# A hybrid DeltaNet and attention layer: the second set of inverse loads placed behind the gates' tenth store on SP's queue

## The chip, the cores and the metric

The kernel runs on one core of one Trainium2 chip. The metric is the device time of the launch in microseconds (us): lower is better. The time before is the median of three runs.

## The reference

One layer over 2048 latent tokens of width 1024 and 256 context tokens. A normed, modulated input `h` goes through one wide projection. Two mixers run side by side: a bidirectional chunked gated DeltaNet (4 heads of 128) and windowed attention (8 heads of 64). Each has a SiLU gate (`za`, `zb`), the two are merged by sigmoid gates (`ga`, `gb`) and projected once more.

```python
a_mat = where(strict, einsum('nbhik,nbhjk->nbhij', kb, kc) * decay, 0)
t_mat = triangular_solve(a_mat, eye, lower=True, unit_diagonal=True)   # one inverse for each chunk, head, direction
u = einsum('nbhij,nbhjv->nbhiv', t_mat, vc * bc)
w = einsum('nbhij,nbhjk->nbhik', t_mat, kb * exp(gc))
s_fin, o = lax.scan(step, s0, (u, w, k_dec, g_last, qk, q_dec))        # one state step per chunk, both directions
y = (sigmoid(ga) * (ya @ w_proj_a) + sigmoid(gb) * (yb @ w_proj_b)) @ w_out
```

What matters here is `t_mat`, the inverse of a unit lower triangular matrix for each chunk of 64 tokens, and the gate projections `za`, `zb`, `ga`, `gb`, which are large matrix products that depend on none of that.

## The kernel before

Products are done in a split form: each f32 operand is a high part (`wh`, `hh`) and the rest (`wl`, `hl`), and three matmuls for each of 8 slices of 128 add up to one product, so one product of the gates is 24 matmuls of 128x512.

**The gates.** `gates(range(24), (2, 3), ...)` runs over 24 column tiles m of the gate weights (m below 4 is `za`, below 8 `zb`, below 16 `ga`, the rest `gb`), and for each m over the token groups 2 and 3. In this document product n is the one with n = 2m for group 2 and n = 2m + 1 for group 3. `rest` loads and splits the weights of the next m (`wr` by SP, L241; `wh` on ScalarE, L243; `wl` on VectorE, L246). `rest_run` does product n into one of three PSUM banks (L524 to L526), takes a tanh on ScalarE into one of two SBUF buffers `rt` (L816), and for m below 8 multiplies on VectorE (L818), which is what frees the bank, and stores `rt` from SP's queue (L819). So product n + 3 needs the bank that L818 of product n frees, and the tanh of product n + 2 needs the buffer that store n has left.

**The inverses.** `base` runs twice. Each call loads a set of raw triangular blocks into `N`, 64 partitions for each direction (`nb` at L733, `N` at L734, both on SP's queue; `N` is 1 MB a direction), scales them by beta on VectorE (L737 for the forward half, L739 for the backward half, four instructions each), runs 62 steps of two VectorE instructions each (L747, L749), clears the upper parts on GpSimd (L754) and stores the result (L759). The first set has the context chunks, the first latent blocks of the forward order and the first of the backward one; the second set has the middle blocks, which the scan comes to after eight steps. The steps of both sets share one buffer `btmp`, so the second set's steps run after the first set's. The first set's loads are three `nb` and `N` pairs, since its chunks are not all neighbours; the second set's are two pairs. `base4` does the last blocks, later, and uses the second set's `N` and `nb` again. `mod_gate` sums the residual gate beside the gates: loads `wmg` on SP (L220), scaling on ScalarE (L221), sums on GpSimd (L223).

**What sets the order.** The order of each engine's queue here is made at build time from a simulated timeline: an instruction is put on its engine when the simulation has it ready, the earlier traced first. On the chip each queue then runs in that order. `tc.issue_after(i)` adds no wait: it keeps the instructions of its block behind `i` on `i`'s engine.

Of the kernel before, what the change touches and what calls it, by code (L numbers as in the profile page):

```python
# [32 lines left out]
def hybrid(tc, ins, out, dbg=None, upto=9):  # L33
    nc = tc.nc
    V, S, G, T = nc.vector, nc.scalar, nc.gpsimd, nc.tensor
    ctx = ExitStack()
    with ctx:
        _hybrid(ctx, tc, nc, V, S, G, T, ins, out, dbg, upto)


def _hybrid(ctx, tc, nc, V, S, G, T, ins, out, dbg, upto):
    dma = nc.sync.dma_start
    adma = nc.scalar.dma_start
# [4 lines left out]
    def dscr(name, shape, dt=F32):  # L48
        return dram.tile(shape, dt, name=name)

    def mem(tag):
        if dbg is not None:
            print("MEM", tag, tile.free_sbuf_bytes_per_partition(tc))
# [44 lines left out]
    Nsp = [dscr(f"Nsp{d}", [NC, H, 2, 64, 64]) for d in range(2)]  # L98
    offsp = [dscr(f"offsp{d}", [NC, 64, H, 64]) for d in range(2)]
    QDsp = dscr("QDsp", [NB, 128, H, 128])  # L100
    brT = dscr("brT", [NC, 8, 128])
# [47 lines left out]
    def acc(shape, dt=F32, name="acc"):  # L149
        return psum("acc", shape, dt, name)  # L150
# [101 lines left out]
    if True:  # L252
# [46 lines left out]
        for j in range(2):  # L299
            mps = [psum("acc" if n == 0 else "hps", [4, 512], name=f"mps{n}") for n in range(2)]  # L300
            for k in range(KT):
# [10 lines left out]
                if j == 0 and 2 <= k < 2 + NCB:  # L312
                    c = k - 2
# [169 lines left out]
        for gi in range(8):  # L483
            xts = []
            for j in range(2):
                c = NCB + gi * 2 + j
# [9 lines left out]
            c = NCB + gi * 2  # L496
# [24 lines left out]
    def fm_dense(ps, w, xh, xl, kt=KT):  # L521
        wh, wl = w
        for k in range(kt):
            T.matmul(ps, lhsT=wh[:, k], rhs=xh[:, k], start=k == 0, stop=False)  # L524
            T.matmul(ps, lhsT=wh[:, k], rhs=xl[:, k], start=False, stop=False)  # L525
            T.matmul(ps, lhsT=wl[:, k], rhs=xh[:, k], start=False, stop=k == kt - 1)  # L526
# [183 lines left out]
    def runs(chunks):  # L710

        out = []
        for i, c in enumerate(chunks):
            if out and c == out[-1][1] + out[-1][2]:
                out[-1][2] += 1
            else:
                out.append([i, c, 1])
        return out

    def base(si, npool, pool, fr, bk):  # L720


        n = 8 * len(fr)
        h1 = max(32, n)
        N = npool.tile([128, 64, 64], F32, name="N")
        nb = npool.tile([128, 64], F32, name="nb")
        if n < h1:
            G.memset(N[0:h1], 0.0)
            G.memset(nb[0:h1], 0.0)
        for d, chunks in ((0, fr), (1, bk)):  # L730
            for i0, c, k in runs(chunks):
                p0 = d * h1 + i0 * 8
                dma(nb[p0:p0 + 8 * k], brT[c:c + k, d * 4:d * 4 + 4].rearrange("c h (b t) -> c (h b) t", b=2))  # L733
                dma(N[p0:p0 + 8 * k], Nsp[d][c:c + k].rearrange("c h b r i -> (c h b) r i"))  # L734
        for q in range(4):
            r, w = slice(q * 16, q * 16 + 16), q * 16 + 16
            V.tensor_tensor(N[0:h1, r, 0:w], N[0:h1, r, 0:w],  # L737
                            nb[0:h1, 0:w].unsqueeze(1).to_broadcast([h1, 16, w]), op=ALU.mult)
            V.tensor_tensor(N[h1:h1 + n, r, 0:w], N[h1:h1 + n, r, 0:w],  # L739
                            nb[h1:h1 + n, r].unsqueeze(2).to_broadcast([n, 16, w]), op=ALU.mult)  # L740
        yield 9
        A = N[0:h1 + n]
        for m in range(1, 63):
            tmp = pool.tile([128, 1376], F32, name="btmp")
            r = 63 - m
            tv = tmp[0:h1 + n, :r * m].rearrange("p (r j) -> p r j", j=m)
            V.tensor_tensor(tv, A[:, m + 1:, m].unsqueeze(2).to_broadcast([h1 + n, r, m]),  # L747
                            A[:, m, 0:m].unsqueeze(1).to_broadcast([h1 + n, r, m]), op=ALU.mult)
            V.tensor_tensor(A[:, m + 1:, 0:m], A[:, m + 1:, 0:m], tv, op=ALU.add)  # L749
            yield 2 * (65 + 1.04 * r * m) / 1e3  # L750

        for q in range(4):
            r, w = slice(q * 16, q * 16 + 16), 64 - q * 16
            G.affine_select(A[:, r, q * 16:], A[:, r, q * 16:], pattern=[[1, 16], [-1, w]], base=0,  # L754
                            channel_multiplier=0, compare_op=ALU.is_gt, fill=0.0)
        V.memset(A.rearrange("p r c -> p (r c)")[:, ::65], 1.0)
        for d, chunks in ((0, fr), (1, bk)):
            p0 = d * h1
            dma(Xset[d][si].rearrange("c h b r j -> (c h b) (r j)"), N[p0:p0 + n].rearrange("p r j -> p (r j)"))  # L759
            for ci, c in enumerate(chunks):  # L760
                Xsp[d][c] = Xset[d][si][ci]
        yield 1
# [48 lines left out]
    def rest_run(ev, job, m, gi):  # L811
        w, dst, mm = job
        ps = acc([128, 512], name="rps")
        fm_dense(ps, w, hh[gi], hl[gi])
        t = ev.tile([128, 512], F32, name="rt", bufs=2)
        S.activation(t, ps, AF.Tanh, scale=0.5)  # L816
        if m < 8:
            V.scalar_tensor_tensor(t, t, 1.0, ps, op0=ALU.add, op1=ALU.mult)  # L818
        (dma if m < 8 else adma)(dst[gi][mm], t)  # L819

    BESIDE = 15
    PACE = -1
    NWO = 5
# [6 lines left out]
    def gates(ms, gis, beside=(), by_act=False):  # L830
        beside = iter(beside)
        job = rest(ev, ms[0], by_act)
        for i, m in enumerate(ms):
            for j, gi in enumerate(gis):
                rest_run(ev, job, m, gi)
                if j == 0:
                    nxt = rest(ev, ms[i + 1], by_act) if i + 1 < len(ms) else None
                    next(beside, None)
            job = nxt
# [6 lines left out]
    for si, (fr, bk, np_) in enumerate((([0, 1] + LAT(*range(0, 6)), [0, 1] + LAT(*range(10, 16)), bs),  # L846
                                        (LAT(*range(6, 14)), LAT(*range(2, 10)), bs2))):
        with tc.issue_after(last_conv[0].ins):
            for _ in base(si, np_, bs2, fr, bk):
                pass  # L850
# [14 lines left out]
    def att_consts(pool):  # L865
        kc = pool.tile([128, 2, 2, LC], F32R, name="kc")
        for h in range(2):
            dma(f32(kc[:, h]), Ksp[h, :, :, 0:LC].rearrange("x p t -> p x t"))
        vc = pool.tile([128, NCB, 2, 128], F32R, name="vc")
        dma(f32(vc), Vsp[0:NCB].rearrange("c p h x -> p c h x"))  # L870

        band = pool.tile([128, 9, 128], F32, name="band", bufs=1)
        G.memset(band, 0.0)
        for j, m in ((0, 6), (2, 7), (5, 6)):
            dma(band[:, j], ins["k_mats"][m])
        band = band.rearrange("p b k -> p (b k)")
        sk = pool.tile([128, 2, 8], F32, name="sk")
        dma(sk[:, 0], ins["sink"].to_broadcast([128, 8]))
        V.tensor_scalar(sk[:, 1], sk[:, 0], -1.0, None, op0=ALU.mult)
        return kc, vc, sk, band  # L880
# [291 lines left out]
    with tc.tile_pool(name="scan", bufs=1, side="right", reuse_waits="tile") as scp:  # L1172
# [5 lines left out]
        with tc.high_priority(first):  # L1178
            scan(scp, scl, cs, first)
        gates(list(range(4, BESIDE)), (1, 0))  # L1180
        mem("r1b")
# [91 lines left out]
    attention(al, ar, [4 * gi + j for gi in (1, 2, 0, 3) for j in range(4)], att_consts(al))  # L1273
    gates(list(range(BESIDE, 24)), (1, 0))
    wp, last = [], {}
# [24 lines left out]
    with tc.tile_pool(name="p4h", bufs=1, side="right", reuse_waits="tile") as hr, \  # L1300
# [168 lines left out]
        with tc.manual_schedule(engines={EN.DVE, EN.Activation, EN.Pool, EN.PE}):  # L1469
# [19 lines left out]
            for k in range(len(seq) + 1):  # L1489
                u, i = divmod(k, 7)  # L1490
# [95 lines left out]
```

## Time and profile before

| | us |
|---|---|
| median of 3 runs | 2004.53 |
| lowest, highest | 1999.01, 2006.01 |
| the profiled execution | 2006.64 |
| its span, first to last instruction | 2004.9 |

The mean granted clock of TensorE is 0.984 of full speed in the profiled execution. TensorE is busy for 96% of the span, VectorE for 75%, ScalarE for 40%, GpSimd for 35%. The shares are averages over stages with different limits: the gates over groups 2 and 3 run from about 629 to 911 us, with the inverses beside them, and the scan follows.

### The profile page before, as it was taken

To read this page: it belongs to the slowest core of one execution; us is meant where nothing else is said; L and a number is where in the kernel's file an instruction comes from. 1 tells how busy PE (TensorE), PEld (TensorE's weight loads), DVE (VectorE), ACT (ScalarE), POOL (GpSimd) and SP (SyncE) were. 2 spreads that over 40 slices of the span, in tenths; PEclk is the share of its full clock that TensorE was granted. 3 is DMA by queue.
4 is the path that set the end of the run, shared out by engine and by line. 5 is a ranking of instruction groups with operands and counts; after the bars stand their busy time and mean duration, and the time that the engine had idled before them with its cause. 6 is when DMAs were issued, how large, how long until landed. Compare 5 with 4: busy or idle time off the path is not lost. (4 is left out here: it accounts for less than half of the span.)

```text
span 2004.9 us, 32107 instructions
## 1 busy us (share of the span) xinstructions
PE 1921.2 (96%) x10947; PEld 1611.0 (80%) x10947; DVE 1509.2 (75%) x2871; ACT 807.4 (40%) x1998; POOL 692.6 (35%) x768
## 2 busy tenths in 40 slices
PE   6999999989999999999999999999989999999998
PEld 3888888779998778877888888788768888877786
DVE  6979766667776899999777776535587777747888
ACT  5755545554444322111222233224675655532221
POOL 1652210225543202004222233323456444420675
PEclk8999999999999999999999999999999999999999
DMA  7542326764546733537887777755355555456454
GB/s 252 175 127 94 98 87 154 184 162 157 161 143 166 189 113 113 142 90 216 225 255 221 224 213 217 193 176 165 126 187 173 176 162 165 129 165 211 137 169 136
DMA packets 387704, 333.12 MB, mean 166 GB/s; under 512 B 83993, under 2 KB 307537, under 8 KB 386901
## 3 DMA queue, kind: packets, MB, share of 16 engines
q1 hardware_dynamic: 352244, 288.60, 49.9%
q10 hardware_dynamic: 35296, 42.48, 6.0%
q8 instruction: 87, 1.43, 0.3%
q14 instruction: 77, 0.62, 0.1%
HBM read 220.28 MB, written 109.13 MB: 164 GB/s over the span
## 5 line engine op out<-in xcount | busy, mean ns | idle before, releaser
L524 PE MATMUL rps<-hh,wh 128*128 128x512 f32 x768 | 309.6, 403 | 5.0 <-DVE rt L818 3.8
L526 PE MATMUL rps<-hh,wl 128*128 128x512 f32 x768 | 309.0, 403 | 0.0
L525 PE MATMUL rps<-hl,wh 128*128 128x512 f32 x768 | 307.7, 401 | 0.0
L563 DVE SCALAR_TENSOR_TENSOR cacc<-y,cw,cacc 128x512 f32<-128x512 f32 (+1 forms) x224 | 163.2, 750 | 22.9 <-ACT cacc L561 18.9
L524 PEld LDWEIGHTS rps<-hh,wh 128*128 128x128 f32 x768 | 145.7, 190 | 39.8 <-DVE rt L818 4.3
L525 PEld LDWEIGHTS rps<-hl,wh 128*128 128x128 f32 x768 | 145.8, 190 | 32.7
L526 PEld LDWEIGHTS rps<-hh,wl 128*128 128x128 f32 x768 | 145.7, 190 | 32.8
L524 PE MATMUL lps<-hh,wh 128*128 128x512 f32 (+1 forms) x448 | 171.6, 383 | 0.2 <-ACT y L634 0.2
L525 PE MATMUL lps<-hl,wh 128*128 128x512 f32 (+1 forms) x448 | 171.3, 382 | 0.0
L526 PE MATMUL lps<-hh,wl 128*128 128x512 f32 (+1 forms) x448 | 171.2, 382 | 0.0
L945 DVE TENSOR_TENSOR pl<-pt,ph 128x512 fp32r<-128x512 f32 x156 | 105.4, 685 | 41.9 <-ACT ph L943 41.2
L943 ACT CAST ph<-pt 128x512 fp32r<-128x512 f32 x156 | 90.2, 585 | 109.9 <-PE pt L941 76.8
L917 DVE CUSTOM_DVE_ANT_0 pr<-sc,band,sk 128x640 f32<-128x640 f32 (+1 forms) x128 | 106.6, 862 | 34.4 <-PE sc L913 18.3
L816 ACT ACTIVATE rt<-rps 128x512 f32<-128x512 f32 x96 | 57.3, 596 | 181.6 <-PE rps L526 167.8
L749 DVE TENSOR_TENSOR N<-N,btmp 128x62 f32<-128x62 f32 (+30 forms) x124 | 117.2, 945 | 3.0
L747 DVE TENSOR_TENSOR btmp<-N 128x62 f32<-128x62 f32 (+30 forms) x124 | 116.6, 940 | 3.1
L927 POOL TENSOR_SCALAR pr<-pr,sm 128x640 f32<-128x640 f32 (+1 forms) x128 | 99.7, 799 | 55.5 <-DVE sm L925 39.0
L919 ACT ACTIVATE pr<-pr,sm 128x640 f32<-128x640 f32 (+1 forms) x128 | 104.0, 815 | 20.4 <-DVE sm L917 20.4
L246 DVE TENSOR_TENSOR wl<-wr,wh 128x512 fp32r<-128x512 f32 x120 | 92.7, 786 | 24.7 <-POOL wh L245 21.9
L1231 PE MATMUL pps<-yh,wph 128*128 128x512 f32 x256 | 104.8, 411 | 4.3 <-ACT yh L1211 2.2
L245 POOL TENSOR_SCALAR wh<-wr 128x512 fp32r<-128x512 f32 x72 | 48.6, 690 | 170.3 <-PE lps L525 97.2
L1232 PE MATMUL pps<-yl,wph 128*128 128x512 f32 x256 | 100.9, 396 | 0.0
(374 smaller groups left out, 5044.2 us busy)
## 6 DMA issues: line engine op xcount, KB each, us to landing
wr<-in_w_in_dram SPq DMA_DIRECT2D x120, 256.0 KB
kw<-Ksp SPq DMA_DIRECT2D x28, 384.0 KB
x<-vsp SPq DMA_DIRECT2D x36, 256.0 KB
k<-ksp SPq DMA_DIRECT2D x34, 256.0 KB
kT<-kTsp SPq DMA_DIRECT2D x34, 256.0 KB
wm<-in_w_mod_dram SPq DMA_DIRECT2D x16, 512.0 KB
xt<-in_x_dram SPq DMA_DIRECT2D x16, 512.0 KB
dtl<-Dsp SPq DMA_DIRECT2D x32, 256.0 KB
```

The costliest lines, as they stand in the source:

```text
L524: T.matmul(ps, lhsT=wh[:, k], rhs=xh[:, k], start=k == 0, stop=False)
L525: T.matmul(ps, lhsT=wh[:, k], rhs=xl[:, k], start=False, stop=False)
L526: T.matmul(ps, lhsT=wl[:, k], rhs=xh[:, k], start=False, stop=k == kt - 1)
L563: V.scalar_tensor_tensor(a, y[:, t:t + n], cw[:, m, t:t + 1], a, op0=ALU.mult, op1=ALU.add)
L747: V.tensor_tensor(tv, A[:, m + 1:, m].unsqueeze(2).to_broadcast([h1 + n, r, m]), A[:, m, 0:m].unsqueeze(1).to_broadcast([h1 + n, r, m]), o ...
L749: V.tensor_tensor(A[:, m + 1:, 0:m], A[:, m + 1:, 0:m], tv, op=ALU.add)
L917: V.tensor_tensor_reduce(s_, ps[:, o:768], band[:, b0:b0 + W + 256], -0.125, sk[:, 1, hd:hd + 1], ALU.add, ALU.min, sm[:, h, 1:2])
L919: S.activation(s_, s_, AF.Exp, scale=-1.0, bias=sm[:, h, 1:2], accum_out=sm[:, h, 2:3])
L927: G.tensor_scalar(p[:, h, :W + 256], p[:, h, :W + 256], sm[:, h, 3:4], 1.0, op0=ALU.mult, op1=ALU.mult)
L945: V.tensor_tensor(pl, pt, f32(ph), op=ALU.subtract)
L1231: T.matmul(ps, lhsT=wh[:, k, ms], rhs=hs[k], start=k == 0, stop=False)
L1232: T.matmul(ps, lhsT=wh[:, k, ms], rhs=ls[k], start=False, stop=False)
```

## The change

The loads of the second set (`si` = 1) are traced under an order edge to the tenth entry of a new list, `stored`, to which `rest_run` appends each of its stores. The tenth entry is store 9: m = 4, group 3, the second of the stores to `zbsp`, issued from SP. The edge keeps the second set's two `nb` loads and two `N` loads behind that store in SP's queue. The first set is untouched, no operation is added or removed, and no semaphore wait is added. The order of all queues is planned anew at the build.

```diff
         for d, chunks in ((0, fr), (1, bk)):
             for i0, c, k in runs(chunks):
                 p0 = d * h1 + i0 * 8
-                dma(nb[p0:p0 + 8 * k], brT[c:c + k, d * 4:d * 4 + 4].rearrange("c h (b t) -> c (h b) t", b=2))
-                dma(N[p0:p0 + 8 * k], Nsp[d][c:c + k].rearrange("c h b r i -> (c h b) r i"))
+                with tc.issue_after(stored[9].ins) if si else nullcontext():
+                    dma(nb[p0:p0 + 8 * k], brT[c:c + k, d * 4:d * 4 + 4].rearrange("c h (b t) -> c (h b) t", b=2))
+                    dma(N[p0:p0 + 8 * k], Nsp[d][c:c + k].rearrange("c h b r i -> (c h b) r i"))
@@
-        (dma if m < 8 else adma)(dst[gi][mm], t)
-
+        stored.append((dma if m < 8 else adma)(dst[gi][mm], t))
+
+    stored = []
```

## Rows read from the trace of the kernel before

**Rows 1.** The page: busy time, share of the span, instructions.

```profile
PE 1921.2 (96%) x10947; PEld 1611.0 (80%) x10947; DVE 1509.2 (75%) x2871; ACT 807.4 (40%) x1998; POOL 692.6 (35%) x768
```

**Rows 2.** Stretches of 25 us: length, engines' busy time, granted clock, DMA share, GB/s.

```profile
650.00:675.00 25.00, 21.98 (x95) 17.35 (x93) 17.11 (x29) 5.99 (x10) 2.54 (x2) 1.00 0.94 230
675.00:700.00 25.00, 24.18 (x92) 19.36 (x93) 24.49 (x31) 9.13 (x16) 9.69 (x8) 0.86 0.54 159
700.00:725.00 25.00, 25.00 (x109) 20.12 (x108) 24.66 (x28) 5.29 (x9) 0.86 (x1) 1.00 0.29 85
925.00:950.00 25.00, 23.49 (x162) 18.95 (x161) 23.94 (x31) 3.28 (x7) 13.55 (x14) 1.00 0.92 270
975.00:1000.00 25.00, 23.48 (x165) 19.92 (x163) 18.09 (x35) 4.99 (x14) 6.25 (x7) 1.00 1.01 252
1250.00:1275.00 25.00, 20.41 (x125) 18.21 (x124) 15.10 (x40) 6.50 (x27) 8.63 (x15) 0.88 0.79 219
```

**Rows 3.** Timeline, TensorE: start, length, line, operation, idle before and its releaser.

```profile
675.82 0.79 PE L524 MATMUL rps<-hh,wh 128*128 128x512 f32 x1 [3.84 <-DVE rt L818]
```

**Rows 4.** Stretches of 2.5 us around that stall.

```profile
673.50:676.00 2.50, 0.18 (x1) 0.18 (x2) 2.47 (x4) 2.37 (x5) 2.18 (x1) 0.79 0.14 48
676.00:678.50 2.50, 2.50 (x6) 1.97 (x7) 2.47 (x3) 0.34 (x1) 1.69 (x3) 0.50 0.39 105
678.50:681.00 2.50, 2.50 (x7) 1.97 (x6) 2.50 (x5) 0.72 (x1) 1.17 (x1) 0.50 0.74 210
```

**Rows 5.** Timeline, ScalarE: tanh of products 2, 3, 4, 10, 12, 24.

```profile
649.78 0.60 ACT L816 ACTIVATE rt<-rps 128x512 f32<-128x512 f32 x1 [0.46 <-PE rps L526]
661.91 0.59 ACT L816 ACTIVATE rt<-rps 128x512 f32<-128x512 f32 x1
672.30 0.60 ACT L816 ACTIVATE rt<-rps 128x512 f32<-128x512 f32 x1 [9.81 <-DMA zasp<-rt]
701.22 0.60 ACT L816 ACTIVATE rt<-rps 128x512 f32<-128x512 f32 x1 [2.53 <-PE rps L526]
712.42 0.60 ACT L816 ACTIVATE rt<-rps 128x512 f32<-128x512 f32 x1 [2.78 <-PE rps L526]
780.77 0.60 ACT L816 ACTIVATE rt<-rps 128x512 f32<-128x512 f32 x1 [2.24 <-PE rps L526]
```

**Rows 6.** Timeline, SP's queue: start, time to issue, line, transfer.

```profile
656.59 0.65 SPq L733 DMA_DIRECT2D nb<-brT  x1
657.35 0.51 SPq L734 DMA_DIRECT2D N<-Nsp  x1
657.90 0.59 SPq L733 DMA_DIRECT2D nb<-brT  x1
658.86 0.49 SPq L734 DMA_DIRECT2D N<-Nsp  x1
660.15 0.33 SPq L819 DMA_DIRECT2D zasp<-rt  x1
...
678.61 0.66 SPq L776 DMA_DIRECT2D nb<-brT  x1
...
705.33 3.89 SPq L819 DMA_DIRECT2D zbsp<-rt  x2
```

**Rows 7.** Timeline, VectorE: scaling of both sets, with the waits for their loads.

```profile
646.65 3.02 DVE L737 TENSOR_TENSOR N<-N,nb 64x256 f32<-64x256 f32 x4 [6.27 <-DMA N<-Nsp]
656.36 3.04 DVE L739 TENSOR_TENSOR N<-N,nb 64x256 f32<-64x256 f32 x4 [4.88 <-DMA N<-Nsp]
665.84 3.01 DVE L737 TENSOR_TENSOR N<-N,nb 64x256 f32<-64x256 f32 x4
672.01 3.04 DVE L739 TENSOR_TENSOR N<-N,nb 64x256 f32<-64x256 f32 x4 [2.77 <-DMA N<-Nsp]
```

**Rows 8.** Timeline, VectorE: multiplies of products 2, 4, 10, 11; weights of m = 12.

```profile
659.43 0.69 DVE L818 SCALAR_TENSOR_TENSOR rt<-rt,rps 128x512 f32<-128x512 f32 x1
675.08 0.69 DVE L818 SCALAR_TENSOR_TENSOR rt<-rt,rps 128x512 f32<-128x512 f32 x1
708.18 0.68 DVE L818 SCALAR_TENSOR_TENSOR rt<-rt,rps 128x512 f32<-128x512 f32 x1
715.15 0.68 DVE L818 SCALAR_TENSOR_TENSOR rt<-rt,rps 128x512 f32<-128x512 f32 x1
772.25 0.69 DVE L246 TENSOR_TENSOR wl<-wr,wh 128x512 fp32r<-128x512 f32 x1
```

**Rows 9.** Timeline, VectorE: first and last of five waits for weight casts, 860 to 920.

```profile
866.33 0.69 DVE L246 TENSOR_TENSOR wl<-wr,wh 128x512 fp32r<-128x512 f32 x1 [0.64 <-ACT wh L243]
911.18 1.08 DVE L246 TENSOR_TENSOR wl<-wr,wh 128x512 fp32r<-128x512 f32 x1 [1.33 <-POOL wh L245]
```

**Rows 10.** Timeline, SP's queue: the second set's result stored.

```profile
967.95 1.15 SPq L759 DMA_DIRECT2D Xsp<-N  x2
```

## Prediction

> **What bounds the kernel now.** I read the page first: TensorE is busy 96% of the span and VectorE 75% [rows 1], so what a change off TensorE can give is a stall of TensorE, and I looked for stalls near the moved loads. The stretches of 25 us show one: from 700 us on TensorE does 109 gate matmuls in 25 us, but only 95 and 92 in the two stretches before [rows 2]. That is 31 matmuls missing at 25 / 109 = 0.229 us each, **7.1 us lost**. Of these 3.84 us are a wait for a free bank [rows 3]; the rest, about 3.3 us, is the clock: the granted clock stands at 0.50 (1.2 of 2.4 GHz) for two stretches of 2.5 us after the idle one, with 6 and 7 matmuls in each [rows 4].
>
> Next, why. Product 7 waited for the multiply of product 4 at 675.08 [rows 8], which waited for its tanh at 672.30, and that had stood 9.81 us for an `rt` buffer, held by store 2 [rows 5]. Store 2 was issued at 660.15, directly behind the second set's four loads [rows 6], and its buffer came free 12.15 us later, at 672.30. The second set's backward load, issued at 658.86, let VectorE go on at 672.01 [rows 6, 7]. So the store waited out the 2 MB ahead of it. Store 2 was also late: product 2 was ready at 649.78 and multiplied at 659.43 [rows 5, 8], since VectorE stood 6.27 and 4.88 us for the first set's loads [rows 7].
>
> The third thing to see is VectorE. It is busy 24.5 and 24.7 us of 25 from 675 to 725 [rows 2], so what it has to do there is as tight as TensorE. Only from 866 us does it wait for weights cast behind TensorE (five waits) [rows 9].
>
> **What the change moves.** Four loads leave SP's queue at 656.59 and come behind store 9, the first of the two at 705.33 [rows 6]. On SP they cost from 656.59 to 659.35, 2.8 us of issue, and no engine waits on that by itself. Passed on SP are stores 2 to 9, eight weight loads and eight of `mod_gate`'s. `base4`'s `nb` load at 678.61 needs the buffer that the second set's scaling reads, so it and the GpSimd memset ahead of it move back too; both belong to work after 968 us [rows 6, 10], and I cost them at nothing. The second set itself has time: its result is stored at 967.95 [rows 10], its steps follow the first set's anyway, and the scan reads it eight steps later.
>
> Step 1, the old place. Without the 2 MB ahead of it store 2 lands in time, the tanh of product 4 goes when the product is ready, and the stall and the slow clock behind it go: **7.1 us for TensorE**, if nothing else is late.
>
> Step 2, VectorE. The scaling, 3.01 + 3.04 = 6.05 us [rows 7], is moved and not saved. Saved is the wait of 2.77 us inside it. Between 666 us and the new place VectorE is some 8.8 us earlier; behind the new place it is earlier by 2.77 - w, where w is what it waits for the loads at the new place.
>
> Step 3, how far TensorE can run ahead of VectorE. Products end 5.60 us apart, from (712.42 - 701.22) / 2 [rows 5]. Product 14 needs the bank that the multiply of product 11 frees at 715.15 + 0.68 = 715.83; product 13 ends at 712.42 + 5.60 = 718.02. Slack 2.2 us. Product 24 starts at 780.77 - 5.60 = 775.17 and needs the low weights of m = 12, done at 772.94 [rows 5, 8]: again 2.2 us. Product 13, whose bank is freed by product 10's multiply at 708.86, starts at 712.42 and has 3.6. So TensorE can lead by 2.2 us more than VectorE gains: its own gain is the smaller of 7.1 and 2.2 + 2.77 - w, that is **5.0 - w**.
>
> Step 4, w. It is not in the trace. The rows give 0 (forward half of the second set) to 6.27 + 4.88 = 11.15 us (both halves of the first set) [rows 7]. The loads are the same kind as those of the second set now: 1 MB a direction, two directions, VectorE full. Other traffic is less (a DMA share of 0.29 against 0.94 [rows 2]), but the plan still expects them sooner than the chip gives them, in three of four halves. I take the nearest row, 2.77 us. That leaves TensorE 5.0 - 2.77 = 2.2 us. With w = 0 it is 5.0; with w = 11.15 it is -6.2, and a stall of that size brings a slow clock as in step 1, 3.3 more: -9.5.
>
> Step 5, whether it lasts. From 866 us VectorE follows TensorE [rows 9], so it takes up the lead of TensorE. In 925 to 1000 us TensorE loses 1.5 us in each of two stretches to the scan's chain [rows 2]; that chain starts when the gates are done, so it moves along. I carry the 2.2 us to the end in full.
>
> The profiled execution took 2006.64 us, 2.1 above the median. Against it the sum is 2006.64 - 2.2 = 2004.4; against the median, 2004.53 - 2.2 = **2002.3**, which I forecast as 2002.
>
> **A rule that speaks against it.** The Trainium skill, page DMA: Bandwidth & Descriptors, section Rules for kernel authors, says to issue a DMA early, compute, and wait for it late. By that rule the old place is the better one. This trace has the price of the early place, 7.1 us, which the rule doesn't count; what a late place costs is rival C below, and by it alone the time would be 2014. The same page's section on queues, rings and completion order says that each DMA engine takes descriptors in ring order, so a store cannot pass loads that were queued ahead of it; the 672.01 and 672.30 above agree.
>
> **Rivals.** B, the whole 7.1 us: the plan puts the scaling late enough (w near 0), and the new order also moves product 11's multiply and the weights of m = 12 ahead of it. For it: the DMA engines are less loaded at 705. Against: slack of 2.2 us in two places with VectorE full. 2004.53 - 7.1 = 1997.4.
>
> C, slower: the late loads stop VectorE. Place: the scaling, about 10 us behind store 9, with all multiplies and weight splits in VectorE's queue behind it. Price: w as for the first set, 11.15 us, gives -9.5 and 2014. It decides from w = 5.0 up. For it: three of four halves waited. Against it: the two halves of the second set waited 2.77 in all.
>
> D, the new plan: the queues are made from a simulated timeline, so a shift of VectorE work by 40 us can change the order of everything behind, scan and attention included. The stretch at 1250 us alone lost 4.6 us of TensorE's time and 25 x 0.12 = 3.0 more by a clock of 0.88 [rows 2]. Two such stalls less, or two more, on top of the forecast give 2002.3 - 15.2 = 1987 or 2002.3 + 15.2 = 2017.5. Nothing in the trace says which way.
>
> E, nothing gained: the stall moves with the loads. Store 10 now stands behind 2 MB, and the tanh of product 12 waits for it. With VectorE 8.8 us earlier store 10 goes at about 700 and lands 12.15 later, at 712; tanh and multiply end at 713.5, and the bank is wanted when product 14 ends, 712.42 + 2 x 5.60 - 7.1 = 716.5. So it would be hidden by 3 us, unless VectorE is late too. 2004.5.
>
> **How the numbers follow.** Forecast A (gain of 0 to 5 us) 0.40, B 0.17, C 0.10, E 0.08, D for the better 0.17, D for the worse 0.08. A measurement of this kernel can tell some 0.5%, 10 us, from no change. Within it lie A, B, E and half of C: 0.70. Faster is D's better half, 0.17; slower is D's worse half and half of C, 0.13. The range takes in A, B, E and most of C, and reaches into the nearer half of D's better side: 1992 to 2013, with some 0.18 left out.
>
> **What would show it.** Step 1: the stretch 650 to 700 us has some 218 matmuls instead of 187, a clock of 1.00, and no tanh waits near 10 us for a store. Step 2 and 4: L737 and L739 of the second set stand after the tenth store, with a wait that is w. Step 3: short waits of TensorE for L818 or for L246 between 705 and 780 us, of 7.1 less what was gained. Step 5: the last gate product ends earlier by as much as the span is shorter. It is wrong if the stall stays at 672, if w is over 5 us, or if most of the difference arises after 1000 us, where the edit does nothing by itself.

## The result and the profile after

| | before | after |
|---|---|---|
| median, us | 2004.01 (11 runs) | 2009.04 (11 runs) |
| lowest, highest, us | 1999.01, 2006.85 | 2005.01, 2018.37 |
| ratio of after to before, 95% interval | | 1.0040, 1.0026 to 1.0054 |
| the profiled execution, its span, us | 2006.64, 2004.9 | 2017.17, 2015.2 |

The change costs 0.4%, some 8 us. That is inside the 0.5% named as "same" and inside the range, but the forecast was a gain of 2.2 us, and the interval excludes a gain. The sign was wrong.

The two spans differ by 10.3 us. I split this at two marks of the trace: the start of product 0 and the tanh of product 47, the last of the gates' stage.

| stage of the profiled execution, us | before | after | difference |
|---|---|---|---|
| start to product 0 | 629.19 | 634.45 | +5.3 |
| product 0 to tanh of product 47 | 281.5 | 285.4 | +3.9 |
| from there to the end | 1094.2 | 1095.4 | +1.2 |

The first row isn't the edit's. The order on TensorE, VectorE, ScalarE and GpSimd is the same in both kernels up to there, and in the twelve kernels below this start lay anywhere from 624.0 to 630.0 us. The profiled execution of after is also a long one, 8.1 us above its median. What is left, 5.1 us, is a little under the interval of 5.2 to 10.8 us (0.26% to 0.54% of 2004), and the two medians by themselves are 5.0 us apart. A sum over stages of one execution and a ratio over all runs differ by several us in this kernel. Below I take places from the traces and verdicts from the ratios.

In the page, what VectorE, ScalarE and GpSimd do is as before, and TensorE is busy 1.9 us longer in a longer span [rows 1]:

```profile
PE 1923.1 (95%) x10947; PEld 1610.1 (80%) x10947; DVE 1508.0 (75%) x2871; ACT 805.9 (40%) x1998; POOL 691.5 (34%) x768
```

The stretches of 25 us of after (length, busy time of the engines, granted clock, DMA share, GB/s) answer to [rows 2]. The stall at 672 is gone (109 matmuls, not 95, to 675 us), but now 80 follow where there were 92, and from 700 to 750 us 100 and 99:

```profile
650.00:675.00 25.00, 25.00 (x109) 20.11 (x108) 17.82 (x28) 6.64 (x12) 3.99 (x3) 1.00 0.84 211
675.00:700.00 25.00, 20.63 (x80) 16.23 (x79) 24.52 (x29) 7.64 (x13) 7.39 (x5) 0.86 0.42 128
700.00:725.00 25.00, 23.19 (x100) 18.33 (x98) 20.62 (x26) 4.47 (x8) 0.00 (x0) 1.00 0.64 155
725.00:750.00 25.00, 24.72 (x99) 19.84 (x100) 24.63 (x27) 5.37 (x10) 0.14 (x1) 0.93 0.36 118
```

Two waits of TensorE for a bank stand there, at product 8 and at product 14; [rows 3] was at product 7. In after, lines from L735 on are one higher: tanh L817, multiply L819, store L820. The timeline of TensorE in after:

```profile
687.20 0.79 PE L524 MATMUL rps<-hh,wh 128*128 128x512 f32 x1 [4.37 <-DVE rt L819]
725.28 0.50 PE L524 MATMUL rps<-hh,wh 128*128 128x512 f32 x1 [2.09 <-DVE rt L819]
```

Counted from the start of product 0, product 7 starts at 42.62 us (before: 46.62) and product 9 at 60.58 (before: 60.62). So before lost 6.8 us over products 6 and 7; after gained exactly these and lost them again over products 7 and 8. Product 13 still starts at 82.98 in after and 83.02 in before. Products 13 and 14 then take 7.85 and 7.26 us instead of 5.60, and product 16 starts at 103.69 instead of 99.82. That is 3.9 us lost, and the difference is still 3.9 at product 47.

**The first stall.** Product 8 waits for the multiply of product 5, which starts at 686.47. Two engines are late ahead of it. The first is ScalarE: product 5 ended at 671.6, and its tanh ran only at 682.05. Ahead of it in ScalarE's queue stand three scalings of `mod_gate` (L221), each waiting for its own load of `w_mod`. The timeline of ScalarE in after:

```profile
675.47 0.73 ACT L221 ACTIVATE wmg<-wmg,silc 128x512 f32<-128x512 f32 x1 [3.14 <-DMA wmg<-in_w_mod_dram]
676.91 0.72 ACT L221 ACTIVATE wmg<-wmg,silc 128x512 f32<-128x512 f32 x1 [0.72 <-DMA wmg<-in_w_mod_dram]
680.39 0.72 ACT L221 ACTIVATE wmg<-wmg,silc 128x512 f32<-128x512 f32 x1 [2.75 <-DMA wmg<-in_w_mod_dram]
681.02 1.12 ACT L243 CAST wh<-wr 128x512 fp32r<-128x512 f32 x2
682.05 0.59 ACT L817 ACTIVATE rt<-rps 128x512 f32<-128x512 f32 x1
```

The second is VectorE, and it is the one that ends last. The tanh was done at 682.64, but VectorE still had work queued ahead of the multiply. From the multiply of product 2, at 664.69, to that of product 5 it has no gap over 0.04 us. The end of that stretch, in the timeline of VectorE in after:

```profile
683.53 1.75 DVE L246 TENSOR_TENSOR wl<-wr,wh 128x512 fp32r<-128x512 f32 x1
685.21 0.74 DVE L748 TENSOR_TENSOR btmp<-N 128x572 f32<-128x572 f32 x1
685.87 0.68 DVE L246 TENSOR_TENSOR wl<-wr,wh 128x512 fp32r<-128x512 f32 x1
686.47 0.68 DVE L819 SCALAR_TENSOR_TENSOR rt<-rt,rps 128x512 f32<-128x512 f32 x1
```

Some of this work is long: the same split of weights (L246) takes 1.75 us at 683.53 and 0.68 us at 685.87. The longer one runs beside an addition of `mod_gate` on GpSimd (L223). Seven such additions fall into the stretch. The timeline of GpSimd in after:

```profile
666.12 1.29 POOL L223 TENSOR_TENSOR gacc<-gacc,wmg 128x512 f32<-128x512 f32 x1 [18.91 <-ACT wmg L221]
671.26 2.77 POOL L223 TENSOR_TENSOR gacc<-gacc,wmg 128x512 f32<-128x512 f32 x2 [3.85 <-ACT wmg L221]
676.34 2.93 POOL L223 TENSOR_TENSOR gacc<-gacc,wmg 128x512 f32<-128x512 f32 x2 [2.30 <-ACT wmg L221]
681.26 1.79 POOL L223 TENSOR_TENSOR gacc<-gacc,wmg 128x512 f32<-128x512 f32 x1 [1.99 <-ACT wmg L221]
683.39 1.34 POOL L223 TENSOR_TENSOR gacc<-gacc,wmg 128x512 f32<-128x512 f32 x1 [0.34 <-ACT wmg L221]
```

Run e9 below gives the price of this.

**The second stall.** The timeline of SP's queue in after: the four loads do stand behind store 9, and store 10 behind them.

```profile
708.24 0.34 SPq L820 DMA_DIRECT2D zbsp<-rt  x1
708.63 0.67 SPq L734 DMA_DIRECT2D nb<-brT  x1
709.35 0.51 SPq L735 DMA_DIRECT2D N<-Nsp  x1
709.90 0.61 SPq L734 DMA_DIRECT2D nb<-brT  x1
710.56 0.48 SPq L735 DMA_DIRECT2D N<-Nsp  x1
712.00 0.38 SPq L820 DMA_DIRECT2D zbsp<-rt  x1
```

The timeline of VectorE in after. The forward scaling, L738, waits 4.11 us for its load, the backward one, L740, doesn't wait, and the multiply at 724.53 is that of product 11, whose bank product 14 needs:

```profile
718.21 3.02 DVE L738 TENSOR_TENSOR N<-N,nb 64x256 f32<-64x256 f32 x4 [4.11 <-DMA N<-Nsp]
721.16 1.08 DVE L750 TENSOR_TENSOR N<-N,btmp 128x902 f32<-128x902 f32 x1
722.17 1.28 DVE L246 TENSOR_TENSOR wl<-wr,wh 128x512 fp32r<-128x512 f32 x2
723.48 1.03 DVE L740 TENSOR_TENSOR N<-N,nb 64x256 f32<-64x256 f32 x2
724.53 0.69 DVE L819 SCALAR_TENSOR_TENSOR rt<-rt,rps 128x512 f32<-128x512 f32 x1
```

### The profile page after: what moved, and what is told of

The parts are those of the page before. It is cut to its first block, busy times and chain, and to the rows that moved or that the text cites. A ratio compares the mean times of both kernels' runs of the same rounds, so it can differ in the third digit from the quotient of the medians.

```text
span 2015.2 us, 32100 instructions
## 1 busy us (share of the span) xinstructions
PE 1923.1 (95%) x10947; PEld 1610.1 (80%) x10947; DVE 1508.0 (75%) x2871; ACT 805.9 (40%) x1998; POOL 691.5 (34%) x768
## 5 line engine op out<-in xcount | busy, mean ns | idle before, releaser
L817 ACT ACTIVATE rt<-rps 128x512 f32<-128x512 f32 x96 | 57.2, 596 | 185.9 <-PE rps L526 161.2
L919 DVE CUSTOM_DVE_ANT_0 pr<-sc,band,sk 128x640 f32<-128x640 f32 (+1 forms) x128 | 106.6, 862 | 32.6 <-PE sc L915 16.5
L246 DVE TENSOR_TENSOR wl<-wr,wh 128x512 fp32r<-128x512 f32 x120 | 92.4, 786 | 21.5 <-POOL wh L245 16.9
L1235 PE MATMUL pps<-yh,wpl 128*128 128x512 f32 x256 | 101.2, 397 | 0.0
```

The lines of the kernel that those rows point to most:

```text
L919: V.tensor_tensor_reduce(s_, ps[:, o:768], band[:, b0:b0 + W + 256], -0.125, sk[:, 1, hd:hd + 1], ALU.add, ALU.min, sm[:, h, 1:2])
L1235: T.matmul(ps, lhsT=wl[:, k, ms], rhs=hs[k], start=False, stop=k == 3)
```

## The experiments

In what follows p8, p16 and p47 are the starts of products 8, 16 and 47 after product 0, and "tail" is the time from the tanh of product 47 to the last instruction, all in us and from the profile of each kernel. Ratios are to the kernel before, run beside it on the same chip. A tail is one execution's: as the start to product 0 varied by some 10 us over these executions with the work in the same order on TensorE, a difference of a few us between tails is not told from chance.

| kernel | p8 | p16 | p47 | tail | median | before | ratio (95%) |
|---|---|---|---|---|---|---|---|
| before | 55.0 | 99.8 | 275.7 | 1094.2 | | | |
| after | 52.8 | 103.7 | 279.6 | 1095.4 | 2009.04 | 2004.01 | 1.0040 (1.0026 to 1.0054) |
| e1_after_modgate_late | 53.0 | 105.0 | 280.8 | 1100.2 | 2017.86 | 1998.67 | 1.0104 (1.0074 to 1.0134) |
| e2_before_modgate_late | 53.2 | 98.3 | 274.1 | 1092.2 | 1999.60 | 1998.67 | 1.0003 (0.9987 to 1.0018) |
| e3_after_scale_late | 52.6 | 98.9 | 274.8 | 1096.6 | 2000.97 | 1998.67 | 1.0007 (0.9992 to 1.0022) |
| e4_store15 | 52.4 | 100.0 | 275.9 | 1095.7 | 2003.70 | 1998.67 | 1.0020 (1.0004 to 1.0037) |
| e9_after_wmg15 | 48.3 | 94.6 | 270.1 | 1103.1 | 2008.27 | 1997.64 | 1.0051 (1.0035 to 1.0068) |
| e10_before_wmg15 | 54.8 | 99.6 | 274.3 | 1102.1 | 2010.91 | 1997.64 | 1.0074 (1.0057 to 1.0090) |
| e11_scale_late_wmg15 | 48.2 | 93.0 | 267.8 | 1105.4 | 2010.93 | 1997.64 | 1.0070 (1.0052 to 1.0088) |
| e12_store15_wmg15 | 48.2 | 93.0 | 267.8 | 1098.2 | 2005.04 | 1997.64 | 1.0037 (1.0022 to 1.0052) |
| e13_store15_wmg15_pairs | 48.2 | 93.0 | 273.4 | 1098.3 | 2003.99 | 1999.86 | 1.0021 (1.0002 to 1.0040) |
| e14_after_wmg15_pairs | 48.2 | 94.0 | 274.9 | 1090.3 | 2001.18 | 1999.86 | 1.0013 (0.9997 to 1.0030) |
| e15_after_base4_late | 52.9 | 103.4 | 279.3 | 1098.6 | 2014.34 | 1997.92 | 1.0084 (1.0069 to 1.0100) |
| e16_e14_base4_late | 48.2 | 93.9 | 273.0 | 1105.1 | 2010.04 | 1997.92 | 1.0059 (1.0042 to 1.0076) |

**Is the first stall that of `mod_gate`, by its scalings on ScalarE?** First try: begin `mod_gate` four column tiles later, in the kernel after and in the kernel before.

```diff
-        gates(list(range(24)), (2, 3), mod_gate(gp, ones), by_act=True)
+        gates(list(range(24)), (2, 3), chain([None] * 4, mod_gate(gp, ones)), by_act=True)
```

> The changed kernel with the sums of the residual gate begun four column tiles later, so that no scaling of `wmg` stands on ScalarE's queue before product 8. Theory: in the changed kernel the tanh of product 5 went 10 us late because three scalings of `wmg` stood ahead of it and waited 3.14, 0.72 and 2.75 us for their loads; without them the stall ahead of product 8 (4.5 us, and 2.2 of slow clock) goes, products 0 to 9 start 5.6 us apart, and the time falls from about 2009 to 2002 to 2005 (VectorE holds back a part at the second stall). Rival: VectorE is full there, the multiply of product 5 is late by itself, the stall stays, about 2009.

> The kernel before with the sums of the residual gate begun four column tiles later. Theory: the stall ahead of product 7 there comes from store 2 behind the 2 MB of loads, not from ScalarE's order, so it stays (about 3.8 us and a slow clock behind it) and the time is about 2004. Rival: the scalings of `wmg` hold ScalarE here too and the stall goes: about 1997.

This edit says nothing on the cause. In e1 the same three scalings, with waits of 3.91, 0.38 and 3.46 us, still stood ahead of the tanh of product 5, since the order of ScalarE's queue was planned anew and came out alike, and so did VectorE's up to the multiply of product 5. The first stall stayed (p8 at 53.0) and the ratio was worse than that of after. In e2 the stall of before stayed too (3.40 us).

**Is the second stall VectorE's wait, or store 10 behind the loads (rival E)?** e3 leaves the loads and store 10 where after has them, and moves only the scaling behind the multiply of product 15 (`mults` is a list of the multiplies, filled as `stored` is). e4 moves the loads behind store 15.

```diff
-            V.tensor_tensor(N[0:h1, r, 0:w], ...
-            V.tensor_tensor(N[h1:h1 + n, r, 0:w], ...
+            with tc.issue_after(mults[15].ins) if si else nullcontext():
+                V.tensor_tensor(N[0:h1, r, 0:w], ...
+                V.tensor_tensor(N[h1:h1 + n, r, 0:w], ...
```

```diff
-                with tc.issue_after(stored[9].ins) if si else nullcontext():
+                with tc.issue_after(stored[15].ins) if si else nullcontext():
```

> The changed kernel with the scaling of the second set (L738, L740) kept behind the multiply of product 15 on VectorE; its loads stay behind store 9. Theory: the second stall, ahead of product 14, comes from VectorE's wait of 4.11 us and the scaling at a place where multiplies free the banks; it goes (2.2 us and 1.7 of slow clock), the first stall stays, and the time falls by 3.9 to about 2005. Rival: store 10 behind the 2 MB holds the tanh of product 12 and with it the bank; a stall near product 15 stays, about 2009.

> The changed kernel with the loads behind store 15, the last of the gates' stores on SP's queue, instead of store 9. No multiply and no SP store of the gates follows, only the weights' splits. Theory: the first stall stays as in the changed kernel, the second goes, about 2005. Rival: VectorE's wait for the late loads now holds the weights' split of a later column tile and TensorE stalls there by about as much: 2009.

In both the first stall stays (4.24 and 3.98 us) and the second is gone: p16 at 98.9 and 100.0 instead of 103.7. In e3 the tanh of product 12 still waits 10.52 us for the buffer of store 10, and no wait of TensorE follows. The timeline of ScalarE in e3:

```profile
715.86 0.60 ACT L818 ACTIVATE rt<-rps 128x512 f32<-128x512 f32 x1 [10.52 <-DMA zbsp<-rt]
```

So the second stall is VectorE's, and store 10 behind 2 MB is harmless here. With it gone, the ratio of e3 can't be told from 1; that of e4, which has lost it too, is 1.0020 (1.0004 to 1.0037).

**The first stall again, with an edit that acts.** The loads of `w_mod` are put behind store 15, the steps of `mod_gate` begin eight column tiles later, and its last steps follow the gates.

```diff
-                dma(wm, ins["w_mod"][0, k * 128:(k + 1) * 128, cs_])
+                with tc.issue_after(stored[15].ins):
+                    dma(wm, ins["w_mod"][0, k * 128:(k + 1) * 128, cs_])
...
-        gates(list(range(24)), (2, 3), mod_gate(gp, ones), by_act=True)
+        mg = mod_gate(gp, ones)
+        gates(list(range(24)), (2, 3), chain([None] * 8, mg), by_act=True)
+        for _ in mg:
+            pass
```

e9 is this in the kernel after, e10 in the kernel before (which gets the list `stored`, but not the moved inverse loads), e11 in e3 and e12 in e4.

> The changed kernel with the loads of `wmg` kept behind store 15 on SP's queue, so that the scalings of `wmg` can't stand on ScalarE's queue before product 16 (beginning the sums four column tiles later did not move them). Theory: the three waits for `wmg` ahead of the tanh of product 5 are what keeps the first stall alive in the changed kernel; without them that tanh goes 38 to 40 us after the start of product 0 instead of 47.6, product 8 starts 48.2 us after product 0 instead of 52.8, and the second stall, which is VectorE's wait for the moved loads, stays: 1.000 to 1.002 of the kernel before, where the changed kernel is 1.004. Rival: VectorE is full and the multiply of product 5 is late by itself; product 8 starts at 52 to 53 and the ratio stays near 1.004.

> The kernel before with the loads of `wmg` behind store 15. Theory: its stall ahead of product 7 is store 2 behind the second set's 2 MB and has nothing to do with `wmg`; product 7 starts 46 to 47 us after product 0 as before, the ratio is 0.999 to 1.001. Rival: `wmg` is the cause in both kernels; product 7 starts at 42.6 and the ratio is 0.997.

> The changed kernel with both suspects removed: `wmg` loads behind store 15, and the second set's scaling behind the multiply of product 15. Theory: neither stall is left, products 2 to 15 start 5.6 us apart, product 16 starts 93 us after product 0 instead of 103.7 (before: 99.8), and the ratio to the kernel before is 0.996 to 0.998. Rival: VectorE or the loads stop TensorE elsewhere in the stage and product 16 is not before 98.

> The changed kernel with the second set's loads and those of `wmg` both behind store 15. Theory: as with both suspects removed, product 16 starts 93 us after product 0, and the ratio is 0.996 to 0.998. Rival: the 2 MB and the loads of `wmg` now come together and hold the tanhs of products 16 to 20 on ScalarE's queue, which gives a new stall of 4 to 7 us there and a ratio of 1.000 to 1.002.

In e9 the first stall is gone: p8 at 48.3, so the 6.8 us that before lost are kept. TensorE is busy without a gap from 650 to 700 us at the full clock.

The place of product 8 is the one expected, but e9 doesn't show that the scalings on ScalarE were the cause, since with the loads of `w_mod` the additions on GpSimd went too. No run takes away one of the two and leaves the other; the trace separates them. From product 0 to the multiply of product 5 VectorE has the same 57 instructions in the same order in after and in e9. The 28 of them from the multiply of product 2 up to that of product 5, in after and then in e9 (length; busy time of TensorE, its weight loads, VectorE, ScalarE, GpSimd; granted clock, DMA share, GB/s):

```profile
664.69:686.47 21.78, 18.14 (x78) 14.27 (x76) 21.23 (x28) 9.59 (x16) 9.90 (x7) 0.97 0.44 134
```

```profile
659.05:673.81 14.76, 14.76 (x65) 11.73 (x64) 14.21 (x28) 3.04 (x5) 0.00 (x0) 1.00 0.31 91
```

VectorE's busy time falls by 7.0 us, and all of it lies in seven instructions, each 0.8 to 1.1 us longer in after beside one of GpSimd's seven additions. So the multiply of product 5 goes 45.4 us after product 0 in e9 and 52.0 in after, and product 8 needs its bank at 48.2. ScalarE's waits are the next late item and not the last: the weights that the split at 683.53 reads were cast by 681.62, so without the additions alone the multiply would have ended some 1.5 us too late for product 8 instead of 4.5 (an estimate: 681.62, then 1.87 us to the multiply as in e9, and its 0.68).

In e10 the stall of before stays, 3.61 us, one product earlier, at product 6. Here it is the second set's scaling alone: the tanh of product 3 was done at 658.49, but its multiply stands on VectorE behind L739, which starts after 2.57 us idle (for which the trace names no releaser). The tanh of product 4 waits for store 2's buffer as in [rows 5], behind that. The timelines of VectorE and ScalarE in e10:

```profile
664.60 3.02 DVE L739 TENSOR_TENSOR N<-N,nb 64x256 f32<-64x256 f32 x4 [2.57 <-issue]
668.47 0.67 DVE L820 SCALAR_TENSOR_TENSOR rt<-rt,rps 128x512 f32<-128x512 f32 x1
```

```profile
670.63 0.60 ACT L818 ACTIVATE rt<-rps 128x512 f32<-128x512 f32 x1 [12.14 <-DMA zasp<-rt]
```

The two kernels together separate the causes. Before's stall belongs to the inverse loads at their old place, and moving those is what removes it (e10 against e9). After's first stall belongs to the work of `mod_gate` beside it (after against e9), and by the trace to its additions on GpSimd. Each alone is enough to stop TensorE, so removing one shows the other. With both gone, and without the second stall, e11 and e12 have no stall left before product 16 and reach product 47 at 267.8 us, 7.9 us earlier than before. 6.8 us of these are there at product 16; step 1 of the prediction forecast 7.1 for the old place alone.

Yet all four are slower than before, by 0.4 to 0.7%, and none of the four ratios is the one expected: the tail is 4 to 11 us longer. `mod_gate` now ends later. In e12, the best of them, the scan's two directions start apart: the first products `vps` of the forward and of the backward direction start 9.0 us apart, against 1.0 us in before. The timelines of TensorE, first e12, then before:

```profile
924.65 1.13 PE L1106 MATMUL vps<-x,mw 128*128 128x128 f32 x8 [0.54 <-ACT mw L1039]
933.61 1.16 PE L1106 MATMUL vps<-x,mx 128*128 128x128 f32 x8
```

```profile
935.54 1.05 PE L1099 MATMUL vps<-x,mw 128*128 128x128 f32 x8
936.54 1.06 PE L1099 MATMUL vps<-x,mx 128*128 128x128 f32 x8
```

The scan's last state comes 402.3 us after the tanh of product 47 in e12, and 390.1 in before. What sets the directions apart I can only argue: the last steps of `mod_gate` hold a PSUM bank that the backward direction's first products need. In e12 the sum is written to that bank at 901.03 and VectorE reads it only at 931.58; in before it is read at 860.2.

**`mod_gate` late, but done sooner.** e13 is e12 and e14 is e9, each with two steps of `mod_gate` per column tile.

```diff
-        gates(list(range(24)), (2, 3), chain([None] * 8, mg), by_act=True)
+        gates(list(range(24)), (2, 3), chain([None] * 8, (next(mg, None) for _ in mg)), by_act=True)
```

> As the kernel with the second set's loads and those of `wmg` behind store 15, but the residual gate's sums take two steps for each column tile from m = 8 on, so that both are done well before the scan. Theory: the two kernels without stalls were slower in all because the second sum of the residual gate, which borrows the PSUM bank of the scan's backward direction, came only at 931 us, when the scan had begun, and put the two directions 8 us apart; done early, the scan stage takes again about 1094 us from the last gate tanh to the end, the gates stage keeps its 8 us (product 47 at 268 us after product 0), and the ratio to the kernel before is 0.995 to 0.998. Rival: the scan stage is longer for another reason, a different order of its queues, and stays at 1098 to 1105: a ratio of 0.999 to 1.004.

> The changed kernel (second set behind store 9) with `wmg` behind store 15 and two steps of the residual gate's sums for each column tile. Theory: only the second stall is left, and short (product 47 at 270 us after product 0), the scan stage as in the kernel before: 0.996 to 0.999. Rival: the scan stage stays at 1100 and more: 1.001 to 1.005.

The last state comes after 393.1 and 388.6 us again, which agrees with that argument. But the second sum's additions on GpSimd now fall between 774 and 800 us, and near 805 us TensorE waits for VectorE's low weights (2.67 and 2.24 us; that the additions are the reason is not shown); of the lead at p16, 6.8 and 5.8 us, 2.3 and 0.8 are left at p47. The timeline of TensorE in e14:

```profile
803.98 0.50 PE L528 MATMUL rps<-hh,wl 128*128 128x512 f32 x1 [2.24 <-DVE wl L248]
```

e14 is 0.13% from before, not to be told from it: the moved loads cost nothing any more, and gain nothing. Both ratios are above what was expected.

**The rest of the loss, in the scan.** In after, `base4`'s scaling on VectorE waits 7.21 us for its loads, and TensorE waits 3.96 us for `moff`, which stands behind it. The timelines of VectorE and TensorE in after, then in before:

```profile
1001.33 3.87 DVE L785 TENSOR_TENSOR N<-N,btmp 32x256 f32<-32x256 f32 x4 [7.21 <-DMA N<-Nsp]
...
1005.59 0.27 PE L1030 MATMUL mep<-moff,mx 64*64 64x64 f32 x1 [3.96 <-DVE moff L1027]
```

```profile
988.13 4.71 DVE L784 TENSOR_TENSOR N<-N,btmp 32x256 f32<-32x256 f32 x4 [3.24 <-DMA N<-Nsp]
...
993.23 0.27 PE L1028 MATMUL mep<-moff,mx 64*64 64x64 f32 x1 [1.52 <-DVE moff L1025]
```

e15 (in after) and e16 (in e14) begin `base4` one scan step later.

```diff
-            if 2 <= st < NC - 2:
+            if 3 <= st < NC - 2:
```

> The kernel after, with base4's steps begun one scan step later (from the fourth step of the scan, not the third); the gates stage is not touched, so product 8 should start near 52.8 and product 47 near 279.6 us after product 0, as in the profile of after. Theory (base4's scaling stands on VectorE ahead of `moff` and waits there 7.21 us for its N loads, and TensorE waits 3.96 us for `moff` at 1005.59): the scaling stands later, its loads are there, the wait of TensorE for `moff` is under 2 us, and from the last gate tanh to the end it takes 2 to 4 us less than the 1095.4 of after; ratio 1.002 to 1.003 to the kernel before. Rival (that wait is hidden by the scan's own chain, so the end does not move): 1095 from the last gate tanh to the end and the ratio of after, 1.004. Second rival (base4 then ends late and the last scan steps wait for its result): over 1098, ratio over 1.005.

> The kernel after with the weights of mod_gate behind the sixteenth store in pairs, and base4 begun one scan step later as well. Theory (the wait ahead of `moff`, 4.55 us of TensorE at 994.33 without the shift, is the rest of the loss): that wait is under 2 us, from the last gate tanh to the end it takes 1086 to 1089 us against 1090.3, and the ratio is 0.998 to 1.000. Rival (the wait is hidden): 1090 and 1.001. Second rival (base4 too late for the last scan steps): over 1093, ratio over 1.003.

The theory's first half holds: the wait for `moff` is gone in both. Its second half fails: both are slower than the kernels that they were made from (1.0084 against 1.0040, 1.0059 against 1.0013), as the second rival said. The scan's last state comes 5.0 and 16.5 us later, and new waits stand late in the scan; e15's timeline of TensorE has this one:

```profile
1288.05 0.27 PE L1025 MATMUL myp<-my,moff 64*64 64x64 f32 x1 [2.96 <-DVE my L1021]
```

So in these two kernels the early place of `base4` is worth more than the wait it causes; that the late waits are the reason is argued, not shown. No kernel here beats the one before.

## Why the prediction was wrong

**What bounds the kernel, and step 1.** The loads at their old place are the cause of the old stall: with them gone product 7 starts at 42.62 instead of 46.62, and by the starts of products the price is 6.8 us, where I counted 7.1. One link of the chain was read wrong. The multiply of product 4 at 675.08 didn't wait for its tanh, which was done at 672.90 [rows 5]; it stood on VectorE behind the second set's backward scaling, which began at 672.01 and lasted 3.04 us [rows 7, 8]. The tanh held by store 2 came second. Both hang on the moved loads, so the price stands, but the prediction looked along the path of the store and not at VectorE, where the next stall came from.

**Step 2, and the condition of step 1, are what failed.** Step 1 holds "if nothing else is late", and step 2 has VectorE "some 8.8 us earlier" between 666 us and the new place. After gained no such lead: the multiply of product 5 goes 50.46 us after product 0 in before and 52.02 in after, 1.6 us later. Its line in the timeline of VectorE in before:

```profile
679.66 0.68 DVE L818 SCALAR_TENSOR_TENSOR rt<-rt,rps 128x512 f32<-128x512 f32 x1
```

Two terms are missing in the sum. The new order fills the place of the scaling with steps of the first set: 21 of their instructions stand between the multiplies of products 2 and 5 in after, 13 in before; the eight more take some 5.3 us at the lengths they have in e9. And GpSimd's additions cost VectorE 7.0 us there, against 2.3 in before, where three of the seven fall into that stretch; I had put `mod_gate` at nothing. That is some 10 us against the 8.8 saved, on an engine that the prediction itself called as tight as TensorE. This is the step that cost the forecast its sign: 7.1 us promised for TensorE, 0.04 kept at product 9. The stretch of 650 to 700 us, where step 1 wanted some 218 matmuls, has 109 + 80 = 189, against 187 before. Of step 2 only the balance of waits for loads held: 2.77 us saved and w = 4.11 paid, 1.34 us later behind the new place.

**Step 3** named the place, product 14 behind the multiply of product 11, and its slack, 2.2 us. From product 0 to that multiply it is 85.96 us in before and 90.08 in after: 4.1 us later, not 1.34. The other 2.8 us are work that the new order puts ahead of it, and work beside GpSimd. The groups of VectorE by line, over just this stretch, in before and then in after (count, busy us, mean ns, idle before):

```profile
L749 DVE TENSOR_TENSOR N<-N,btmp 128x62 f32<-128x62 f32 (+19 forms) x20 | 17.6, 881 | 0.5
L246 DVE TENSOR_TENSOR wl<-wr,wh 128x512 fp32r<-128x512 f32 x12 | 8.0, 682 | 0.0
```

```profile
L750 DVE TENSOR_TENSOR N<-N,btmp 128x62 f32<-128x62 f32 (+21 forms) x22 | 21.2, 965 | 0.5
L246 DVE TENSOR_TENSOR wl<-wr,wh 128x512 fp32r<-128x512 f32 x12 | 9.1, 769 | 0.0
```

Two more additions of the first set's steps and longer instructions make 3.6 + 1.1 = 4.7 us (the steps' multiplies, one more of them, come to about the same sum, 17.9 and 18.1), and half of the backward scaling, which now stands behind the multiply, gives 2.0 back. With no lead of TensorE left from step 1, the stall is 4.1 - 2.2 = 1.9 us; measured 2.09. With the slow clock behind it 3.9 us were lost.

**Step 4**, w = 4.11 instead of 2.77, missed by 1.3 us and is inside its bounds of 0 and 11.15. By the formula it would still have left 5.0 - 4.11 = 0.9 us of gain.

**Step 5** can't be seen at work, as there was no gain to carry; the loss of 3.9 us at p16 is 3.9 at p47. But e11 and e12 speak against it: there 7.9 us were gained in the gates' stage, the tail gave back 11.2 and 4.0, and the ratios are above 1. Their `mod_gate` was moved too, so this doesn't show that a lead alone is lost.

**Rivals.** C came nearest: the late loads stop VectorE and the kernel is slower. Its price was too high (w of 11.15), and its point, w = 5.0, was too high as well, because it counted on the lead of step 1; without it VectorE's lateness decides from 2.2 us. E's mechanism is there, and later than worked out: store 10 was issued at 712.00, and its buffer came free at 723.47, 11.5 us on (11.3 in e3; in after the trace names another releaser for that tanh, in e3 it names the store). It is off the path (e3). B fails as step 1 does. D, a changed order, is what filled VectorE in the gates' stage; in the tail after shows 1.2 us of it, which one execution can't tell from chance. The rule to issue early (the Trainium skill, page DMA: Bandwidth & Descriptors, section Rules for kernel authors) had the sign right. What it gave was 2014 by rival C; here the late place cost 1.34 us more of waiting on VectorE, not 8, and the early place cost 6.8 us, which a second cause took again. Of ring order the prediction says more than the page of the Trainium skill that it cites (DMA: Bandwidth & Descriptors, section Queues, rings and completion order): the page adds that a later descriptor may finish its write before an earlier one, so that a store can't pass the loads is borne out by the rows of stores 2 and 10 and not by the page.

## What to carry to other kernels

When a stall is to be removed, take away its releaser in thought and read what stands next in every queue that feeds the same bank; the price counts only up to the next late item. An operand that comes late is not the cause as long as the engine that takes it has no gap ahead of it: look there for the wait that ends last. Work on an engine that is a third busy (here `mod_gate`'s additions on GpSimd) can still cost the engine that frees the PSUM banks about 1 us an instruction. And an engine with slack of 2 us is moved over it by a wait of 1.3 us if the new order also puts more instructions ahead.

## What the runs showed of the hardware

The granted clock answered short waits. After the idle 4.37 us it stood at 0.50 (1.2 of 2.4 GHz) for a stretch of 2.5 us, as in [rows 4]; after the idle 2.09 us the two stretches of 2.5 us show 0.71 and 0.61, so part of each was at the lower level. I had costed the slow clock only for waits of step 1's size; the 2.09 us wait had 1.8 us of slow clock behind it (3.9 - 2.09). The stretches of 2.5 us in after:

```profile
687.50:690.00 2.50, 2.50 (x7) 1.92 (x7) 2.43 (x5) 0.00 (x0) 0.00 (x0) 0.50 0.96 302
...
725.00:727.50 2.50, 2.22 (x7) 1.78 (x8) 2.44 (x4) 1.24 (x2) 0.09 (x1) 0.71 0.70 233
727.50:730.00 2.50, 2.50 (x9) 1.95 (x8) 2.50 (x3) 0.60 (x1) 0.05 (x1) 0.61 0.02 7
```

VectorE's instructions with two SBUF inputs are longer beside GpSimd's additions: seven of them by 0.8 to 1.1 us each in after, 7.0 us in all, against the same instructions in e9. A multiply of the gates, which reads one of its inputs from PSUM, isn't: in before that of product 4 took 0.69 us at 675.08 [rows 8], with GpSimd adding from 673.82 to 677.68. The timeline of GpSimd in before:

```profile
673.82 3.86 POOL L223 TENSOR_TENSOR gacc<-gacc,wmg 128x512 f32<-128x512 f32 x2 [11.41 <-ACT wmg L221]
```

The Trainium skill, page SBUF — State Buffer, section SBUF: two separate sides, says that the two engines share one pair of ports, which the instruction that starts first holds to its end, where VectorE's has two SBUF inputs and GpSimd's reads SBUF. The rows of the first stall agree: GpSimd started at 683.39 and held it to 684.73, which leaves VectorE's split, started at 683.53, 1.2 us behind; it was 1.07 us longer than the next one. I had costed nothing for `mod_gate`'s additions.
